# The second feed-forward map of two layers: a plain product by 32 contraction tiles against seven half-block products with operand sums on VectorE

## The chip, the cores and the metric

The program runs on one core of one Trainium2 chip. The metric is device microseconds of one execution, as a median over executions; lower is better. One profiled execution gives the trace. Engines are named as in the profile: PE is TensorE, PEld its weight loads, DVE is VectorE, ACT is ScalarE, POOL is GpSimd, SP is SyncE, whose queue issues nearly all DMAs.

## The reference, cut to what matters

The model is one attention block followed by two layers (a state-space mixer and an attention mixer), each with the feed-forward map below, on 1024 positions of width 1024, in fp32. Only the product with `w2` is computed in another way by the change.

```python
D_FF = 4 * D_MODEL                      # 4096, D_MODEL is 1024
def sq_relu_mlp(h, w1, w2):
    return jnp.square(jax.nn.relu(h @ w1)) @ w2
...
for layer in range(DEPTH_2):            # 2
    ...
    h = layer_norm(DN_ALPHA * h + mix, ln_mix_g[layer], ln_mix_b[layer])
    h = layer_norm(DN_ALPHA * h + sq_relu_mlp(h, w_ff1[layer], w_ff2[layer]), ln_ffn_g[layer], ln_ffn_b[layer])
```

## The kernel before

All fp32 products are made of three matmuls: each operand is split into a high part (ACT copies it to fp32r, line 157) and a low part (source minus high part, line 159, on POOL unless the call names DVE), and high x high, high x low and low x high are summed in PSUM. On-chip data lives in 46 pages (48 late in the program) of 128 x 1024 fp32, handed out from a queue: the page that was freed first is taken first, and whoever writes it waits until its last reader is done.

**First map (`ff1`, `ff1_unit`).** It already works by half-blocks: 16 units, each of two 128-row hidden tiles by 1024 positions, each of seven products of 12 matmuls (`product`, line 1276). A unit evicts its sums into two pages h0 and h1 (lines 1325 to 1363), squares them (line 1309) and stores the two tiles in DRAM (`self.dh`, lines 1357 and 1365). The four operand sums of a unit's weights are made on DVE (lines 1292 to 1295).

**Second map (`ff`).** The 32 hidden tiles are contracted in blocks of two (the last block of layer 1 has four). For a block the SP queue loads the hidden tiles and the rows of `w_ff2` (`wload`, line 165), ACT and POOL split them. For each of eight position tiles t, 12 matmuls of 128 x 512 (line 172) fill a PSUM pair of banks, and DVE adds it into a page z[t] (line 1425). In the last block the layer norm follows tile by tile (`ln`, with POOL's help). In layer 0 the last block is interleaved with transposes of finished tiles (`to_T`) and the first products of the attention mixer (`mla_front`); `mla_tables` computes rotary tables on DVE, ACT and POOL beside block 12. In layer 1 `last_rows` ends the program.

Order of the work: each engine runs its own instructions strictly in one order. The order is fixed when the program is built, by a scheduler that works from the order of the code, priorities and its own estimates. The SP queue is one of these ordered lists: a DMA whose source is not ready holds back every DMA behind it.

Of the kernel before, what the change touches and what calls it, by code (L numbers as in the profile page):

```python
# [59 lines left out]
class Kern:  # L60

    FB = [0, 4, 6, 0, 4, 6, 0, 0]
    FLAG = 5
# [1325 lines left out]

    def ff(self, X, units, layer, last):  # L1390
# [5 lines left out]
        z = []  # L1396
        f0 = 0
        for b, n in enumerate(sizes):
            end = b == len(sizes) - 1
            hid = [self.wload(self.dh[f0 + f]) for f in range(n)]  # L1400
            ws = [self.wload(i["w_ff2"][layer, f0 + f]) for f in range(n)]
            if b == len(sizes) - self.TB and not last:
                self.mla_tables()
            if end:
                gb = self.ln_rows(2 + layer)
                if not last:
                    self.psum(big=self.FB, tr=[2], kv=[4, 5], kq=[6, 7])
                    front, ahead = self.mla_front(), deque()
                    next(front)
            for t in range(8):  # L1410
                sl = slice(t * 128, (t + 1) * 128)
                if b == 0:
                    z.append(self.pg())
                    nc.sync.dma_start(z[t].t, self.dzr[t])
                ps = self.big()
                if last and end and t == 7:
                    self.last_rows(z[t].t, ps, hid, ws, sl, gb)
                    break
                for f in range(n):
                    (h, l), w = hid[f], ws[f]  # L1420
                    for a, c in ((h, 0), (h, 1), (l, 0)):
                        for hf in range(2):
                            cs = slice(hf * 512, (hf + 1) * 512)
                            self.mm(ps[:, cs], a[:, sl], w[c][:, cs], f == 0 and a is h and c == 0, f == n - 1 and a is l)
# [1 line left out]
                if end:
                    self.ln(z[t].t, gb, nc.gpsimd if t in ((5, 6) if last else (0, 1, 2, 3, 4, 5, 6)) else None)
                    if last:
                        nc.sync.dma_start(self.out.rearrange("(k t) d -> k t d", t=8)[:, t, :], z[t].t)
                    else:  # L1430
                        self.dump("h2", [(np.s_[t::8, :], z[t].t)])
                        nc.sync.dma_start(self.dres[:, t, :], z[t].t)
                        hT = [self.pg((128, 8, 128), F32R) for _ in range(2)]
                        self.to_T(z[t].t, *([p.t] for p in hT))
                        self.fr(z[t])
                        ahead.append((t, hT))
                        if len(ahead) > self.FLAG:
                            front.send(ahead.popleft())
            self.fr(*(p for w in hid + ws for p in w.pg))
            f0 += n  # L1440
# [1 line left out]
        if last:
            return
        for a in ahead:
            front.send(a)
        return front.send(None)

    def last_rows(self, z, ps, hid, ws, sl, gb):
# [3 lines left out]
        st, mv = self.sm(12, "st"), self.sm(2, "mv")  # L1452
        n = len(hid)
        for hf in range(2):
            cs = slice(hf * 512, (hf + 1) * 512)
            for f in range(n):
                (h, l), w = hid[f], ws[f]
                for a, c in ((h, 0), (h, 1), (l, 0)):
                    self.mm(ps[:, cs], a[:, sl], w[c][:, cs], f == 0 and a is h and c == 0, f == n - 1 and a is l)
            V.scalar_tensor_tensor(z[:, cs], ps[:, cs], IALPHA, z[:, cs], MUL, ADD)  # L1460
            V.bn_stats(st[:, hf * 6:hf * 6 + 6], z[:, cs])
# [373 lines left out]
```

## Time and profile before

| | |
|---|---|
| median of 3 runs | 3126.07 us (3124.21 to 3129.84) |
| the profiled execution's own time | 3125.07 us |
| its span in the trace | 3123.3 us |
| PE busy | 3002.7 us, 96% of the span |
| DVE, ACT, POOL busy | 54%, 35%, 44% of the span |
| mean granted TensorE clock | 0.983 of full |

Busy shares are over the whole program. What a stage costs is read from the engine whose wait ends last there. Times in the trace count from the start of the span.

### The profile page before, as it was taken

Reading aid. Unit: us, or ns where it says so; the run is one execution under the profiler, and the core shown is the slowest. Engines: PE = TensorE matmul, PEld = TensorE weight load, DVE = VectorE, ACT = ScalarE, POOL = GpSimd, SP = SyncE. Lnnn points to the kernel's source line nnn. Section 1 sums busy time; section 2 is a strip of 40 time slices with the busy share of each in tenths; the row PEclk is TensorE's granted clock in tenths of the full one; section 3 lists DMA queues with packets and bytes.
Section 4 is the critical chain, followed back from the end, with each engine's and each line's share of the span. In section 5 each row is a group of like instructions: output and inputs, shape, how many; then the busy total and the mean of one; then the engine's idle time right before and its main releaser. Section 6 shows DMA issues by size and latency. Waiting matters only on the chain.

```text
span 3123.3 us, 38309 instructions
## 1 busy us (share of the span) xinstructions
PE 3002.7 (96%) x14764; PEld 2471.2 (79%) x14764; DVE 1688.7 (54%) x2506; ACT 1106.9 (35%) x1723; POOL 1388.0 (44%) x831
## 2 busy tenths in 40 slices
PE   7999889999998899999999999999999899999998
PEld 6777667777777788878888888888998788888887
DVE  7555547755289401764444464756554854444446
ACT  4332247765233311332232211336662432232210
POOL 5454637644522233334456443513353354464442
PEclk9999999999999999999999999999999999999999
DMA  4353463476644112223353222110123233262211
GB/s 165 131 176 111 129 200 96 124 221 205 203 136 141 41 61 108 101 101 109 114 223 118 111 97 73 70 46 33 45 94 123 104 116 111 109 251 92 108 68 74
DMA packets 166168, 369.96 MB, mean 118 GB/s; under 512 B 21697, under 2 KB 71105, under 8 KB 165985
## 3 DMA queue, kind: packets, MB, share of 16 engines
q1 hardware_dynamic: 165840, 367.38, 34.8%
q8 instruction: 116, 1.90, 0.3%
q14 instruction: 68, 0.55, 0.1%
q10 hardware_dynamic: 144, 0.13, 0.0%
HBM read 252.90 MB, written 106.17 MB: 115 GB/s over the span
## 4 chain that ended last, share of the span: by engine, by line
PE 77%; DVE 11%; DMA 4%; issue 2%; POOL 2%; ACT 2%; SPq 0%; DVEq 0%; POOLq 0%; ACTq 0%
PE ps L172 56%; PE ps L1276 18%; DMA dr<-p 2%; POOL p L159 1%; PE ps L1648 1%; DMA p<-dr 1%; DVE p L1032 1%; DMA p<-in_w_ff 1%; DVE p L159 1%; DVE p L1045 1%; PE ps L668 1%; DVE p L498 1%; POOL rsd L180 1%; PE ps L521 1%; ACT p L500 1%
## 5 line engine op out<-in xcount | busy, mean ns | idle before, releaser
L172 PE MATMUL ps<-p,p 128*128 128x512 f32 (+6 forms) x10520 | 2238.1, 373 | 64.4 <-POOL p L159 12.1
L172 PEld LDWEIGHTS ps<-p,p 128*128 128x128 f32 (+2 forms) x10520 | 1790.5, 186 | 440.2 <-issue 50.1
L159 POOL TENSOR_TENSOR p<-p,p 128x1024 fp32r<-128x1024 f32 (+2 forms) x400 | 917.8, 2314 | 997.7 <-ACT p L157 687.9
L157 ACT ACTIVATE p<-p 128x1024 fp32r<-128x1024 f32 (+2 forms) x462 | 423.8, 939 | 935.8 <-DMA p<-in_w_ff 442.9
L1276 PE MATMUL ps<-p,p 128*128 128x512 f32 x2688 | 624.9, 393 | 17.6 <-ACT p L157 12.6
L1276 PEld LDWEIGHTS ps<-p,p 128*128 128x128 f32 x2688 | 506.4, 189 | 133.4 <-ACT p L157 14.1
L1425 DVE SCALAR_TENSOR_TENSOR p<-ps,p 128x1024 f32<-128x1024 f32 x247 | 301.3, 1223 | 335.1 <-PE ps L172 335.1
L180 POOL TENSOR_TENSOR rsd<-rst,nhalf 128x1 f32<-128x1 f32 (+1 forms) x64 | 102.9, 1610 | 219.7 <-DVE rst L178 219.6
L498 DVE CUSTOM_DVE_ANT_0 p<-ps,bw 128x1024 f32<-128x1024 f32 x64 | 77.4, 1220 | 30.6 <-PE ps L172 21.9
L1309 DVE SCALAR_TENSOR_TENSOR p<-p 128x512 f32<-128x512 f32 x96 | 90.3, 940 | 2.4
L1124 DVE SCALAR_TENSOR_TENSOR p<-p,ps 128x1024 f32<-128x1024 f32 x8 | 9.8, 1222 | 143.5 <-ACT p L1123 143.5
L500 ACT ACTIVATE p<-p,m 128x1024 f32<-128x1024 f32 x64 | 73.4, 1148 | 30.6 <-DVE m L498 19.4
L1642 POOL TENSOR_SCALAR p<-p,rz 128x256 f32<-128x256 f32 (+6 forms) x64 | 48.7, 762 | 66.3 <-DVE rz L1641 61.2
L513 POOL TENSOR_TENSOR p<-p,p 128x1024 f32<-128x1024 f32 x32 | 76.8, 2405 | 2.0
L512 POOL TENSOR_SCALAR p<-p,c 128x1024 f32<-128x1024 f32 x32 | 37.0, 1157 | 84.8 <-DMA dr<-p 43.5
L1363 DVE TENSOR_TENSOR p<-p,ps 128x512 f32<-128x512 f32 x32 | 22.0, 688 | 88.7 <-PE ps L1276 88.5
L1329 DVE TENSOR_TENSOR p<-p,ps 128x512 f32<-128x512 f32 x32 | 21.9, 685 | 87.2 <-PE ps L1276 87.2
L665 POOL TENSOR_SCALAR p<-p,rz 128x384 f32<-128x384 f32 x64 | 38.2, 602 | 68.9 <-DVE rz L664 55.1
L1652 DVE TENSOR_TENSOR p<-ps,p 128x512 fp32r<-128x512 f32 (+3 forms) x96 | 50.9, 553 | 32.2 <-ACT p L1651 31.3
L1637 POOL CAST p<-zeros 128x128 fp32r<-128x128 f32 x64 | 18.2, 295 | 105.1 <-PE ps L172 71.0
L1177 ACT ACTIVATE p<-ps 128x512 f32<-128x512 f32 x32 | 17.5, 594 | 130.1 <-PE ps L1176 130.0
L159 DVE TENSOR_TENSOR p<-ps,p 128x1024 fp32r<-128x1024 f32 (+1 forms) x42 | 42.3, 1017 | 38.6 <-ACT p L157 35.7
(252 smaller groups left out, 2396.5 us busy)
## 6 DMA issues: line engine op xcount, KB each, us to landing
p<-dr SPq DMA_DIRECT2D x174, 512.0 KB
dr<-p SPq DMA_DIRECT2D x158, 512.0 KB
p<-in_w_ff SPq DMA_DIRECT2D x136, 512.0 KB
bw<-in_rpbw SPq DMA_DIRECT2D x16, 768.0 KB
dr<-p SPq DMA_DIRECT2D x80, 128.0 KB
p<-p SPq DMA_DIRECT2D x64, 128.0 KB
p<-dr SPq DMA_DIRECT2D x32, 256.0 KB
p<-in_w_glu SPq DMA_DIRECT2D x16, 512.0 KB
```

Source lines behind the costliest of these rows:

```text
L157: nc.scalar.activation(hi, src, AF.Copy, scale=scale)
L159: (eng or nc.gpsimd).tensor_tensor(lo, src, hi.bitcast(F32), SUB)
L172: self.nc.tensor.matmul(out, l, r, start=start, stop=stop)
L180: nc.gpsimd.tensor_tensor(dst, t, self.nhalf[:, :n], ALU.pow)
L498: V.tensor_tensor_reduce(out=s.t, in0=ps, in1=bw[:, 896 - 128 * t:1920 - 128 * t], scale=-1.0, scalar=3e38, op0=ADD, op1=ALU.min, accum_ou ...
L500: A.activation(s.t, s.t, AF.Exp, bias=m[:, c:c + 1], scale=-1.0, accum_out=z[:, c:c + 1])
L513: G.tensor_tensor(p[0].t, p[0].t, p[1].t, ADD)
L1276: self.nc.tensor.matmul(ps, w[a][:, kt, :], x[b][kt // 2].t[:, kt % 2, :], start=start and kt == 0 and (a, b) == (0, 0), stop=kt == 3 and ...
L1309: V.scalar_tensor_tensor(h, h, 0.0, h, ALU.max, MUL)
L1425: V.scalar_tensor_tensor(z[t].t, ps, IALPHA, z[t].t, MUL, ADD)
L1642: G.tensor_scalar(s.t[:, :n], s.t[:, :n], rz, 1.0, MUL, MUL)
L1652: V.tensor_tensor(atl[kq][:, :nb, qi * 128:(qi + 1) * 128], tv, oh.bitcast(F32), SUB)
```

## The change

The second map of each layer is done by seven products of half-blocks instead of eight. Hidden tiles, positions and output columns are each cut in two: the 32 hidden tiles into even and odd, the positions into the first and second 512, the 1024 output columns into halves. With A the hidden activations (blocks by position half and tile parity) and B the rows of `w_ff2`, the sums of blocks of A are made once, in `ff1_unit` (four added DVE instructions of 128 x 512, lines 1368 to 1371 of the new file), and seven blocks instead of four are stored in DRAM (`self.da`). `ff2_ops` makes an operand of a step: it loads the pages, makes the sums of B on DVE, and splits all of them with ACT and DVE (no longer POOL). The steps are 4 sweeps k over 8 pairs of tiles j; k = 0, 1, 2 do two products each (banks P and R, 48 matmuls a step), k = 3 one (24 matmuls). A product's sums stay in four PSUM banks over a whole sweep, and are added into the z pages only at its end; the P banks are carried on from sweep to sweep. Steps are prepared two ahead in the order of the code (`AHEAD`). A sum of B needed in two sweeps goes through DRAM (`dv`, `dt4`). The layer norms of the first four position tiles stand inside sweep 3, without POOL; those of the last four follow the last sweep.

```diff
-    FB = [0, 4, 6, 0, 4, 6, 0, 0]
-    FLAG = 5
-    TB = 4
+    AHEAD = 2
@@ ff1_unit
-        nc.sync.dma_start(self.dh[2 * i + 1], h1.t)
-        self.fr(h1)
+        for p, c in ((1, lo), (2, hi)):
+            nc.sync.dma_start(self.da[p, i], h1.t[:, c])
...
-        nc.sync.dma_start(self.dh[2 * i], h0.t)
-        self.fr(h0)
+        s, t = self.pg(), self.pg()
+        V.tensor_tensor(s.t[:, lo], h0.t[:, hi], h1.t[:, hi], ADD)
+        V.tensor_tensor(s.t[:, hi], s.t[:, lo], h0.t[:, lo], SUB)
+        V.tensor_tensor(h0.t[:, hi], h0.t[:, lo], h0.t[:, hi], SUB)
+        V.tensor_tensor(t.t[:, lo], h1.t[:, lo], s.t[:, hi], SUB)
+        for p, a in ((0, h0.t[:, lo]), (5, h0.t[:, hi]), (3, s.t[:, lo]), (4, s.t[:, hi]), (6, t.t[:, lo])):
+            nc.sync.dma_start(self.da[p, i], a)
+        self.fr(h0, h1, s, t)
@@ new: ff2_ops
+        def sp(p):
+            h = [self.pg((128, 2, 512), F32R) for _ in range(2)]
+            self.split(p.t, h[0].t, h[1].t, eng=V)
+            return h
+        if k == 0:
+            p, q, b11, b21 = a(0), a(1), b(0, 0), b(1, 0)
+            ops = [(sp(p), sp(b11)), (sp(q), sp(b21))]
+            V.tensor_tensor(b21.t, b21.t, b11.t, SUB)
+            nc.sync.dma_start(self.dv[j], b21.t)
+        elif k == 1:
+            b11, b12, q, b22, p = b(0, 0), b(0, 1), a(3), b(1, 1), a(4)
+            V.tensor_tensor(b12.t, b12.t, b11.t, SUB)
+            V.tensor_tensor(b22.t, b22.t, b12.t, SUB)
+            ops = [(sp(p), sp(b22)), (sp(q), sp(b12))]
+        elif k == 2:
+            b12, b22, p, q = b(0, 1), b(1, 1), a(5), a(6)
+            v = self.pg((128, 2, 512))
+            nc.sync.dma_start(v.t, self.dv[j])
...
+            V.tensor_tensor(b12.t, b22.t, b12.t, SUB)
+            ops = [(sp(p), sp(b12)), (sp(q), sp(b22))]
+            V.tensor_tensor(v.t, v.t, b12.t, SUB)
+            nc.sync.dma_start(self.dt4[j], v.t)
+        else:
+            p, v = a(2), self.pg((128, 2, 512))
+            nc.sync.dma_start(v.t, self.dt4[j])
...
+            ops = [(sp(p), sp(v))]
@@ ff
-        self.psum(big=[0, 2, 4, 6])
-        sizes = [2] * 14 + [4] if last else [2] * 16
...
-                V.scalar_tensor_tensor(z[t].t, ps, IALPHA, z[t].t, MUL, ADD)
...
+            for kt in range(2):
+                for x, y in ((0, 0), (0, 1), (1, 0)):
+                    nc.tensor.matmul(ps[c][t], a[x].t[:, kt, t * 128:(t + 1) * 128], b[y].t[:, kt, :],
...
+            for t in range(4):
+                zs = z[4 * r + t].t[:, h * 512:(h + 1) * 512]
+                V.scalar_tensor_tensor(zs, ps[c][t], IALPHA, zs, MUL, ADD)
...
+        for k in range(3):
+            for j in range(8):
+                ops = ahead.popleft()
+                fetch()
+                if k == 1 and j == 0 and not last:
+                    self.mla_tables()
+                for c, op in enumerate(ops):
+                    for t in range(4):
+                        mms(c, op, t, j == 0 and (k == 0 or k == 1 and c == 1), j == 7)
+                    self.fr(*op[0], *op[1])
```

The orders below show three places. Up to the first units of layer 0's first map no engine's order differs. In the changed file line numbers differ: 157 is the split's low part (159 before), 170 the matmul of `mm`, 1276 the first map's products as before, 1310 the square, 1330, 1351, 1357 and 1364 the first map's evictions (1329, 1350, 1356, 1363 before), 1293 to 1296 the sums of weights, 1368 to 1371 the four new sums, 1408, 1436 and 1444 the loads of `ff2_ops`, 1426, 1430, 1431, 1438, 1440 its sums, 1427 and 1441 its stores, 1471 the second map's matmuls, 1479 its evictions.

First place: DVE in the middle of the first map of layer 0. Before, from the last eviction of one unit (L1363) to that of the next:

```order
L1363 TENSOR_TENSOR p_1038_10111<-p_1038_10111,ps 128x512
L1309 SCALAR_TENSOR_TENSOR p_1038_10111<-p_1038_10111 128x512
L1292 TENSOR_TENSOR p_1058_10342<-p_1056_10340 128x512
L1294 TENSOR_TENSOR p_1057_10341<-p_1052_10263,p_1056_10340 128x512
L1293 TENSOR_TENSOR p_1057_10341<-p_1058_10342,p_1052_10263 128x512
L1295 TENSOR_TENSOR p_1058_10342<-p_1052_10263,p_1057_10341 128x512
L1350 TENSOR_TENSOR p_1055_10297<-p_1055_10297,ps 128x512
L1309 SCALAR_TENSOR_TENSOR p_1055_10297<-p_1055_10297 128x512
L1329 TENSOR_TENSOR p_1064_10359<-p_1064_10359,ps 128x512
L1356 TENSOR_TENSOR p_1055_10297<-p_1055_10297,ps 128x512
```

The same in the change:

```order
L1364 TENSOR_TENSOR p_1048_10167<-p_1048_10167,ps 128x512
L1310 SCALAR_TENSOR_TENSOR p_1048_10167<-p_1048_10167 128x512
L1368 TENSOR_TENSOR p_1067_10363<-p_1048_10167,p_1054_10239 128x512
L1369 TENSOR_TENSOR p_1067_10363<-p_1067_10363,p_1048_10167 128x512
L1370 TENSOR_TENSOR p_1048_10167<-p_1048_10167 128x512
L1371 TENSOR_TENSOR p_1068_10364<-p_1054_10239,p_1067_10363 128x512
L1351 TENSOR_TENSOR p_1069_10374<-p_1069_10374,ps 128x512
L1310 SCALAR_TENSOR_TENSOR p_1069_10374<-p_1069_10374 128x512
L1295 TENSOR_TENSOR p_1086_10554<-p_1079_10465,p_1085_10553 128x512
L1293 TENSOR_TENSOR p_1087_10555<-p_1085_10553 128x512
L1357 TENSOR_TENSOR p_1069_10374<-p_1069_10374,ps 128x512
L1330 TENSOR_TENSOR p_1078_10437<-p_1078_10437,ps 128x512
```

The four new sums take the place right behind the unit's last eviction; the weight sums move behind the next eviction, and belong to a later unit than before.

Second place: DVE at the border of the first and second map of layer 0. Before:

```order
L1363 TENSOR_TENSOR p_1155_11227<-p_1155_11227,ps 128x512
L1309 SCALAR_TENSOR_TENSOR p_1155_11227<-p_1155_11227 128x512
L1425 SCALAR_TENSOR_TENSOR p_1169_11365<-ps,p_1169_11365 128x1024
L1425 SCALAR_TENSOR_TENSOR p_1170_11380<-ps,p_1170_11380 128x1024
L1425 SCALAR_TENSOR_TENSOR p_1171_11395<-ps,p_1171_11395 128x1024
```

In the change, from the fourth instruction behind the first map's last eviction (ahead of these stand that eviction, L1364, one split, L157, and one square, L1310):

```order
L157 TENSOR_TENSOR p_1230_11596<-p_1225_11587,p_1229_11595 128x1024
L1426 TENSOR_TENSOR p_1204_11533<-p_1204_11533,p_1203_11531 128x1024
L1368 TENSOR_TENSOR p_1187_11506<-p_1183_11382,p_1186_11448 128x512
L157 TENSOR_TENSOR p_1236_11608<-p_1228_11593,p_1235_11607 128x1024
L1369 TENSOR_TENSOR p_1187_11506<-p_1187_11506,p_1183_11382 128x512
L1370 TENSOR_TENSOR p_1183_11382<-p_1183_11382 128x512
L157 TENSOR_TENSOR p_1234_11604<-p_1226_11589,p_1233_11603 128x1024
L157 TENSOR_TENSOR p_1218_11562<-p_1213_11553,p_1217_11561 128x1024
L1371 TENSOR_TENSOR p_1188_11507<-p_1186_11448,p_1187_11506 128x512
L1426 TENSOR_TENSOR p_1228_11593<-p_1228_11593,p_1227_11591 128x1024
L157 TENSOR_TENSOR p_1232_11600<-p_1227_11591,p_1231_11599 128x1024
L157 TENSOR_TENSOR p_1222_11570<-p_1214_11555,p_1221_11569 128x1024
```

Pages 1201 to 1204 are raw pages of step j = 0, 1213 to 1216 of j = 1, 1225 to 1228 of j = 2; the last row makes the low part that step j = 1 needs, and DVE comes to it behind the four sums of the last unit and splits of step j = 2.

Third place: the SP queue in the middle of the second map of layer 0. Before, loads alone:

```order
L165 DMA p_1258_12271<-in_w_ff 128x1024
L165 DMA p_1261_12381<-dr_8628 128x1024
L165 DMA p_1264_12387<-dr_8628 128x1024
L165 DMA p_1291_12649<-in_w_ff 128x1024
L165 DMA p_1270_12399<-in_w_ff 128x1024
```

In the change, in sweep k = 2 (dr_11525 is `dv`, dr_11526 `dt4`, dr_8628 `da`):

```order
L1441 DMA dr_11526<-p_1432_12850 128x1024
L1408 DMA p_1443_12923<-dr_8628 128x2x512
L1408 DMA p_1444_12925<-dr_8628 128x2x512
L1436 DMA p_1445_12927<-dr_11525 128x1024
L1408 DMA p_1455_12998<-in_w_ff 128x2x512
L1408 DMA p_1467_13073<-in_w_ff 128x2x512
L1441 DMA dr_11526<-p_1445_12927 128x1024
L1408 DMA p_1456_13000<-dr_8628 128x2x512
```

Five loads now stand between two stores, each store waits for a DVE sum of a page that the third of these loads brings, and the loads of the next step stand behind it.

## Rows read from the trace of the kernel before

**Rows 1.** The page: span, busy time by engine, granted clock in 40 slices, chain.

```profile
span 3123.3 us, 38309 instructions
PE 3002.7 (96%) x14764; PEld 2471.2 (79%) x14764; DVE 1688.7 (54%) x2506; ACT 1106.9 (35%) x1723; POOL 1388.0 (44%) x831
PEclk9999999999999999999999999999999999999999
PE 77%; DVE 11%; DMA 4%; issue 2%; POOL 2%; ACT 2%; SPq 0%; DVEq 0%; POOLq 0%; ACTq 0%
```

**Rows 2.** Windows: first map, second map, layer 0's end; then layer 1's maps.

```profile
core 0: us, PE busy (x) PEld busy (x) DVE busy (x) ACT busy (x) POOL busy (x), PEclk, DMA share, GB/s
1360.00:1600.00 240.00, 240.00 (x1055) 197.68 (x1054) 111.63 (x139) 73.70 (x101) 115.36 (x50) 1.00 0.32 114
1640.00:1840.00 200.00, 200.00 (x878) 164.43 (x877) 91.64 (x76) 44.60 (x42) 107.56 (x46) 1.00 0.32 115
1966.00:2055.00 89.00, 85.05 (x519) 81.22 (x518) 54.19 (x118) 34.17 (x64) 43.16 (x35) 1.00 0.18 67
2500.00:2740.00 240.00, 239.90 (x1050) 196.78 (x1049) 113.53 (x139) 73.32 (x102) 114.73 (x51) 1.00 0.32 113
2775.00:3060.00 285.00, 285.00 (x1256) 235.31 (x1255) 130.16 (x107) 55.02 (x52) 135.40 (x57) 1.00 0.27 99
```

**Rows 3.** Waits of PE, second map of layer 0, then behind it.

```profile
PE ps L172 <- DVE p L1425: 1.2, 1, 1.2
...
PE ps L172 <- DVE p L1425: 1.7, 1, 1.7
PE ps L1164 <- DVE rst L178: 1.6, 1, 1.6
PE ps L1164 <- DVE mv L1144: 0.7, 1, 0.7
```

**Rows 4.** Timeline of PE where layer 1's second map starts, and DVE at its end.

```profile
2757.60 4.24 PE L172 MATMUL ps<-p,p 128*128 128x512 f32 x18
2761.68 5.61 PE L1276 MATMUL ps<-p,p 128*128 128x512 f32 x24
...
3113.26 0.69 DVE L1460 SCALAR_TENSOR_TENSOR p<-ps,p 128x512 f32<-128x512 f32 x1
```

**Rows 5.** Groups by form, 1400 to 1600 us (first map): busy us, mean ns, idle before.

```profile
L1276 PE MATMUL ps<-p,p 128*128 128x512 f32 x880 | 200.7, 390 | 0.0
L159 POOL TENSOR_TENSOR p<-p,p 128x1024 fp32r<-128x1024 f32 x31 | 78.2, 2550 | 21.3 <-ACT p L157 21.3
L1293 DVE TENSOR_TENSOR p<-p,p 128x512 f32<-128x512 f32 x10 | 17.8, 1781 | 0.0
L1294 DVE TENSOR_TENSOR p<-p,p 128x512 f32<-128x512 f32 x10 | 6.8, 685 | 0.0
```

**Rows 6.** Timeline of DVE, one unit of the first map.

```profile
1502.59 0.69 DVE L1363 TENSOR_TENSOR p<-p,ps 128x512 f32<-128x512 f32 x1 [3.48 <-PE ps L1276]
1503.31 0.69 DVE L1309 SCALAR_TENSOR_TENSOR p<-p 128x512 f32<-128x512 f32 x1
...
1510.10 0.69 DVE L1350 TENSOR_TENSOR p<-p,ps 128x512 f32<-128x512 f32 x1 [1.88 <-ACT p L1346]
1510.82 0.86 DVE L1309 SCALAR_TENSOR_TENSOR p<-p 128x512 f32<-128x512 f32 x1
1516.34 0.69 DVE L1329 TENSOR_TENSOR p<-p,ps 128x512 f32<-128x512 f32 x1 [4.65 <-PE ps L1276]
```

**Rows 7.** Timeline of DVE, page-wide two-operand work with POOL idle.

```profile
1332.07 1.21 DVE L1243 TENSOR_TENSOR p<-p,p 128x1024 f32<-128x1024 f32 x1
1334.41 1.21 DVE L159 TENSOR_TENSOR p<-p,p 128x1024 fp32r<-128x1024 f32 x1
```

**Rows 8.** Groups by form, 1640 to 1960 us (second map, layer 0).

```profile
L1425 DVE SCALAR_TENSOR_TENSOR p<-ps,p 128x1024 f32<-128x1024 f32 x119 | 145.0, 1224 | 163.2 <-PE ps L172 163.2
L159 POOL TENSOR_TENSOR p<-p,p 128x1024 fp32r<-128x1024 f32 x58 | 138.4, 2411 | 146.8 <-PE ps L172 81.6 <-ACT p L157 64.7
L157 ACT ACTIVATE p<-p 128x1024 fp32r<-128x1024 f32 x52 | 55.2, 1062 | 204.4 <-DMA p<-in_w_ff 132.6 <-DMA p<-dr 40.9 <-PE ps L172 26.4
```

**Rows 9.** DMA: the crowded border (window row), a store of 2 KB rows in 40 slices of 222.8 to 227 us, a lone load in the chain.

```profile
1612.00:1640.00 28.00, 27.91 (x121) 21.95 (x119) 9.86 (x11) 12.14 (x14) 16.17 (x7) 1.00 1.01 392
...
GB/s 0 0 0 0 0 0 0 0 0 332 390 351 371 449 390 332 390 410 410 351 390 332 98 0 0 0 0 0 0 0 0 0 0 0 0 0 0 0 0 0
...
1307.97 4.19 DMA p<-in_w_ff
```

**Rows 10.** Groups by form, whole span: DVE sums beside busy POOL.

```profile
L1243 DVE TENSOR_TENSOR p<-p,p 128x1024 f32<-128x1024 f32 x16 | 25.7, 1627 | 0.0
```

**Rows 11.** Window in which `mla_tables` runs on DVE.

```profile
1847.00:1867.00 20.00, 18.40 (x21) 1.00 0.22 80
```

More of the change, by code (lines that the diff above doesn't have):

```diff
@@ L1393, in ff @@
         self.ff1(X, units, layer)
-        self.psum(big=[0, 2, 4, 6])
-        sizes = [2] * 14 + [4] if last else [2] * 16
[L1396 to L1424, printed above, removed]
-                V.scalar_tensor_tensor(z[t].t, ps, IALPHA, z[t].t, MUL, ADD)
[L1426 to L1440, printed above, removed]
@@ new lines, in ff, with fetch, mms @@
+        z = [self.pg() for _ in range(8)]
+        self.dv, self.dt4 = self.dr([8, 128, 2, 512]), self.dr([8, 128, 2, 512])
+        self.psum(**{f"{n}{t}": [4 * c + t] for c, n in enumerate("PR") for t in range(4)})
+        ps = [[self.bank(f"{n}{t}") for t in range(4)] for n in "PR"]
+        steps, ahead = [(k, j) for k in range(4) for j in range(8)], deque()
+        def fetch():
+            if steps:
+                ahead.append(self.ff2_ops(layer, *steps.pop(0)))
+        def mms(c, op, t, start, stop):
+            a, b = op
+            for kt in range(2):
+                for x, y in ((0, 0), (0, 1), (1, 0)):
+                    nc.tensor.matmul(ps[c][t], a[x].t[:, kt, t * 128:(t + 1) * 128], b[y].t[:, kt, :],
+                                     start=start and kt == 0 and (x, y) == (0, 0), stop=stop and kt == 1 and x == 1,
+                                     skip_group_check=True)
@@ new lines, in ff, with done, turn @@
+        gb = self.ln_rows(2 + layer)
+        self.psb["tr"] = cycle([4])
+        if not last:
+            front = self.mla_front()
+            next(front)
+        tail, queue = [], deque()
+        def done(t):
+            if last:
+                nc.sync.dma_start(self.out.rearrange("(k t) d -> k t d", t=8)[:, t, :], z[t].t)
+            else:
+                self.dump("h2", [(np.s_[t::8, :], z[t].t)])
+                nc.sync.dma_start(self.dres[:, t, :], z[t].t)
+        def turn(t):
+            hT = [self.pg((128, 8, 128), F32R) for _ in range(2)]
+            self.to_T(z[t].t, *([p.t] for p in hT))
+            self.fr(z[t])
+            queue.append((t, hT))
@@ new lines, in ff @@
+        for j in range(8):
+            (op,) = ahead.popleft()
+            fetch()
+            if last and j > 3:
+                tail.append(op)
+            else:
+                for t in range(4):
+                    mms(0, op, t, False, j == 7)
+                self.fr(*op[0], *op[1])
+            if j % 2 == 0:
+                self.ln(z[j // 2].t, gb)
+                done(j // 2)
+            elif not last:
+                turn(j // 2)
+        st = [self.sm(12, "sth") for _ in range(4)]
@@ new lines, in ff @@
+        for t in range(4):
+            V.bn_stats(st[t][:, 6:12], z[4 + t].t[:, 512:])
+        if last:
+            for t in range(4):
+                for n, op in enumerate(tail):
+                    mms(0, op, t, False, n == 3)
+                zs = z[4 + t].t[:, :512]
+                V.scalar_tensor_tensor(zs, ps[0][t], IALPHA, zs, MUL, ADD)
+                if t < 3:
+                    self.ln(z[4 + t].t, gb, st=st[t])
+                    done(4 + t)
+            self.last_rows(z[7].t, st[3], gb)
+            return
@@ L1441, in ff, with last_rows @@
+        add(0, 1, 0)
+        self.psum(tr=[4, 2], kv=[6, 0], kq=[7, 1])
+        for t in range(4, 8):
+            self.ln(z[t].t, gb, st=st[t - 4])
+            done(t)
+            front.send(queue.popleft())
+            if t > 4:
+                turn(t - 1)
+        turn(7)
+        for a in queue:
+            front.send(a)
         self.fr(*gb)
[L1442 to L1445, printed above, removed]
         return front.send(None)
-    def last_rows(self, z, ps, hid, ws, sl, gb):
+    def last_rows(self, z, st, gb):
@@ L1450, in last_rows @@
         nc = self.nc
         V = nc.vector
[L1452 to L1461, printed above, removed]
+        mv = self.sm(2, "mv")
@@ L1462, in last_rows @@
+        V.bn_stats(st[:, 0:6], z[:, :512])
         V.bn_aggr(mv, st.rearrange("p (n s) -> p n s", s=6))
```

34 lines of the change are left out of this document (30 added, 4 removed).

## Prediction

> **What bounds the kernel now.** I read the page first: PE is busy for 96% of the span at a granted clock of 9 tenths or more in every slice, and 77% of the chain that ended last is PE [rows 1]. The windows say the same of the stages in question: PE is busy for 240 of 240 us in the middle of the first map, 200 of 200 in the second map of layer 0 and 285 of 285 in that of layer 1, all at the full granted clock (2.4 GHz) [rows 2]. The waits of PE in layer 0's second map come to a single one of 1.2 us [rows 3]. So in both second maps time is the number of matmuls times the pitch at which PE takes them, and everything else hides, as long as it keeps up.
>
> The pitch comes from layer 1, where nothing else is mixed in. Its second map starts at 2757.60, 24 matmuls of the first map (5.61 us) lie inside it, and the program's last eviction, DVE's half-page one at 3113.26, starts as the last matmul ends [rows 4]. 3113.26 - 2757.60 - 5.61 = 350.0 us for 32 tiles x 8 positions x 6 = 1536 matmuls: 0.228 us each. The duration of one in the groups (390 ns) is no pitch, since matmuls overlap. The first map, whose matmuls are already of the new form (six or more half-block matmuls in a row into one bank, a new weight load for each), shows 200.7 us for 880, again 0.228 [rows 5]. I take 0.228 for the new matmuls too.
>
> **What is removed on PE.** Seven half-block products of 8 pairs x 4 tiles x 6 = 192 matmuls are 1344 in place of 1536. 192 fewer at 0.228 us is 43.8 us a layer, **-87.6 us** for both. A step of two products is then 48 x 0.228 = 10.9 us, a step of sweep 3 is 5.5 us.
>
> **What the others must do in a step.** DVE first. It loses 128 page evictions a layer at 1.22 us [rows 8], 157 us, and does 28 half-page evictions instead (0.69 us for such an instruction [rows 6], 19 us). It gains all splits and sums. A page-wide two-operand instruction takes 1.21 us when POOL is idle [rows 7], and a mean of 1.63 where POOL works beside it [rows 10]. The splits leave POOL, where they cost 2.41 us each [rows 8], and POOL has almost nothing left in this stage, so I take 1.21. Sweep 0 needs four splits and a sum a step, 6.1 us; sweeps 1 and 2 four splits and two sums, 7.3 us; sweep 3 two splits, 2.4 us. All below PE's 10.9 and 5.5, and at 1.63 still (8.2, 9.8, 3.3). ACT makes as many high parts: 4 x 1.06 = 4.2 us a step [rows 8]. The heaviest sweep is k = 1 of layer 0, beside which the rotary tables run: 58 us of steps, at most 18.4 us for the tables [rows 11], 5.5 us of evictions: 82 of 87.5 us. It fits with little to spare.
>
> The row on contention first: in one stretch the same kind of half-page sum takes 1.78 us when it falls on POOL's splits and 0.69 when not [rows 5]. The Trainium skill, GPSIMD Engine Reference, section Specifications, says that GpSimd's SBUF interfaces are shared with VectorE and that DVE instructions with two SBUF inputs contend. By this rule, with which the trace agrees, the second map's sums run at the lone price and the first map's four new ones at up to the stretched one.
>
> DMA. A page of 512 KB moves in 1.34 us at the 392 GB/s of the crowded border [rows 9]. The new pages have rows of 2 KB instead of 4; a store of such rows ran at 330 to 450 GB/s in its 13 full slices [rows 9], some 1.4 us a page, so I take no extra cost for short rows. Sweeps 0 and 1 move five pages a step (6.7 to 7 us), sweep 2 six (8 to 8.4 us), of 10.9. The SP queue in sweep 2 is tighter than its bytes: from one store to the next stand the store itself, two loads, the load of `dv`, the sum that needs it. Four transfers of 1.34 us, the fixed part of a lone load (4.19 less 1.34 [rows 9]), a sum and up to two splits ahead of it: 5.4 + 2.9 + 3.6 = 11.9 us, a microsecond more than a step. Over eight steps that is 8 us, and the work enters the sweep two to three steps (22 to 33 us) ahead, since the pages of a step are free once PE is through with the step four before it (8 of 48 hold z, a step holds 8 and up to 5 raw). I take 0 and keep 8 a layer.
>
> **Bank edges.** At the end of a sweep DVE empties eight banks, 5.5 us. PE needs the P banks again behind the 24 matmuls of R (5.5 us), and P's four evictions take 2.8. So they hide; splits that stand between them can cost something. I take 0.5 us for each of six edges, +3 us (bounds 0 and 3 each).
>
> **First map.** Each unit gets four half-page sums, 2.8 us at 0.69, 7.1 at 1.78. DVE is busy for 111.6 of 240 us there [rows 2], 8.9 of a unit's 19.1. In the unit shown, the last eviction and its square end at 1504.0 and the next eviction is due at 1510.1 [rows 6]; between them stood the weight sums, which the new order moves behind that eviction, at 1511.7, where DVE was idle until 1516.3. The four sums end at 1506.8, or 1511.1 if stretched. Nobody on PE waits for them: their readers come a sweep later. Seven stores of 256 KB replace two of 512 KB, 1.8 MB in 19 us. Cost 0; without that cover, 2.8 us a unit, 88 us in all.
>
> **The border of the maps.** Before, PE lost almost nothing. Now the DVE order has 15 instructions from the last first-map eviction to the low part that step 1 needs: five half-page ones at 0.69 (the eviction and four sums), a square, seven splits and two sums at 1.21: 3.5 + 0.7 + 10.9 = 15.1 us. PE meanwhile has step 0 and twelve matmuls of step 1, 58 to 60 x 0.228 = 13.2 to 13.7 us. It waits 1.4 to 1.9 us. Loads may add: some 20 pages (z, three steps) are 27 us of DMA within a stretch that begins some 20 us ahead of the border. I take 3 us a layer, **+6 us**, bounds 0 and 10 each.
>
> **Ends.** In layer 0 PE waited 4.0 us for DVE's layer norms behind the map and 1.2 inside [rows 3]. Now four tiles are normalised inside sweep 3 and give PE four tiles of mixer products (some 8 us each) while DVE does the other four. I take **-3 us** (0 to -5.2). In layer 1 the last tile's eviction, statistics and output follow the last matmul as before: 0. Sweep 3 there has 14 us of splits, 5.5 of evictions and some 20 of layer norms in 44: it holds.
>
> **Sum**, against the profiled execution's own 3125.1 us: -87.6 + 6 - 3 + 3 = -81.6, so 3043.5. The median of the runs is 1 us above that execution; I predict **3044 us**.
>
> **Rivals.**
> 1. *The SP queue paces sweep 2* (or loads late at the borders pace sweep 0). For: stores wait on DVE with the next loads behind them; 11.9 against 10.9. Against: the lead, and DMA's mean share of 0.32 so far [rows 2]. If a load takes 1 us longer and the lead is gone, 13 us a step: 2.1 x 16 = 33 us, 3077.
> 2. *DVE becomes the bound.* For: it is the engine with all new work, in one fixed order, where one late page holds all. Against: 7.3 of 10.9. At 1.63 only sweep 1 of layer 0 fails: 78 + 18 + 6 = 102 us against 87.5: 3059.
> 3. *The first map pays, and the kernel is slower.* If the four sums delay the evictions so that PE waits for all of them in each of 32 units, 32 x 2.8 = 88 us: 3132. It decides from 2.6 us a unit on. For: POOL works there, and DVE's order is fixed. Against: the idle time around 1508 and 1512 to 1516.
> 4. *The change saves nothing on PE*: a pitch of 0.260 for the new form would eat all. The first map's 0.228 speaks against it.
>
> **How the numbers follow.** Forecast 0.68 (3032 to 3056), rival 1 0.13, rival 2 0.08, rival 3 0.05 with milder forms of it 0.04 (up to 3120), rival 4 0.02. The lower end is everything hidden, 3125.1 - 87.6 - 5.2 = 3032; the upper takes in rivals 1 and 2 and half-way forms of 3: 3031 to 3085. A difference of 0.2% (6 us) is about what a measurement of this kernel can tell. Faster 0.93, same 0.02, slower 0.05.
>
> **What would show it.** Right: 1344 matmuls of line 1471 a layer at 0.228 us and no wait of PE inside sweeps; at the borders one wait of some 2 us for a split on DVE; first-map units still 19.1 us apart. Wrong: waits of PE for splits in sweep 2 with SP waiting for the sum of line 1440 (rival 1); DVE busy all through sweep 1 of layer 0 (rival 2); PE below 240 of 240 in the first map (rival 3); a longer pitch (rival 4).

## The result and the profile after

The changed kernel takes 3057.63 us (median of 4 runs, 3052.07 to 3059.8), the kernel before 3125.76: a ratio of 0.9777 (0.976 to 0.9794). It is faster by 68 us; 3044 was forecast, in 3031 to 3085. The profiled execution took 3052.07 us; its page, span and engines (answers to [rows 1]):

```profile
span 3050.3 us, 38397 instructions
PE 2917.8 (96%) x14380; PEld 2403.1 (79%) x14380; DVE 1879.5 (62%) x2754; ACT 1188.6 (39%) x1810; POOL 1053.8 (35%) x694
```

384 matmuls are gone, DVE has more work and POOL less, as planned. Where the time went is read by stretches. The view of one line gives its matmuls with their first and last start; here the first and the second map of each layer in the changed kernel:

```profile
L1276 PE MATMUL ps<-p,p x1344: 387/389/796, 1304.0 to 1639.9; 128*128 128x512 f32 x192
L1471 PE MATMUL ps<-p,p x1344: 387/389/504, 1636.9 to 1948.8; 128*128 128x512 f32 x192
...
L1276 PE MATMUL ps<-p,p x1344: 387/389/796, 2401.8 to 2733.6; 128*128 128x512 f32 x192
L1471 PE MATMUL ps<-p,p x1344: 387/389/504, 2730.6 to 3041.5; 128*128 128x512 f32 x192
```

A first map is counted from its first to its last start plus one pitch, less 0.228 us for each matmul of the second map inside it: 1639.9 + 0.2 - 1304.0 - 2 x 0.228 = 335.7.

| stretch, us | before | changed | difference | forecast |
|---|---|---|---|---|
| up to the first map of layer 0 | 1305.6 | 1304.0 | -1.6 | 0 |
| first map, layer 0 | 322.8 | 335.7 | +12.9 | 0 |
| second map of layer 0, mixer, up to the first map of layer 1 | 811.3 | 762.1 | -49.2 | -42.3 |
| first map, layer 1 | 323.3 | 331.6 | +8.3 | 0 |
| second map, layer 1 | 350.0 | 308.4 | -41.6 | -39.3 |
| behind the last matmul | 10.3 | 8.6 | -1.7 | 0 |

The forecast puts 43.8 us a layer of saved matmuls, 3 of border and 1.5 of bank edges into the second maps. The first row is the noise of an execution: no instruction there differs, and over the profiled executions below the first map starts between 1301 and 1313 us. So the lengths of maps are compared below, beside medians; the kernel before, run again beside each group of experiments, had medians of 3125.4 to 3129.9 us.

The second maps came out as forecast or better. The first maps, which were to cost nothing, took 21.2 us more than before. The windows of layer 0's first map (changed kernel; answers to the first row of [rows 2]) show PE short of full, and DVE at 156.6 us in place of 111.6:

```profile
1360.00:1600.00 240.00, 234.75 (x1013) 191.08 (x1012) 156.59 (x185) 70.70 (x99) 111.43 (x50) 0.99 0.44 150
```

The chain of waits from 1370 to 1402 us ends in a wait of PE of 2.75 us (start, duration, what):

```profile
1385.44 0.32 SPq L1373
...
1385.81 0.02 SPq L1313
...
1385.86 4.58 DMA p<-in_w_ff
...
1390.53 0.69 DVE p L1294
1391.22 0.60 DVE p L1295
1391.82 2.80 DVE p L1296
1394.62 0.61 DVE p L1364
...
1395.26 2.20 DVE p L1310
...
1397.48 0.70 DVE p L1368
...
1398.20 1.94 DMA dr<-p
1400.13 0.63 ACT p L155
1400.76 0.50 ACT p L1347
...
1401.30 0.79 PE ps L1276
```

Read downwards: the SP queue is through with the stores of a unit's sums (L1373) at 1385.8, and only then issues the load of the next weight tile (L1313). DVE waits for that load, makes the weight sums, and behind them, in its fixed order, the eviction, the square and the first of the four new sums. The store of that page must land (1.94 us) before ACT may write a split into a page that becomes free with it; behind that split stands ACT's eviction L1347, for which PE waits. One of these weight sums took 2.80 us and the square 2.20, where the kernel before has 0.69 for such an instruction that does not fall on POOL's splits [rows 5, rows 6], so DVE's own time is in this wait too. Two links of this loop the change makes longer: loads stand behind stores that wait for the sums (a link of order), and splits get pages that the sums and their stores hold (a link of pages). Which counts, or whether DVE's time alone does, is what most experiments ask.

The loss is not spread evenly over the units. Layer 0's map is 8.0 us behind the kernel before by its 467th matmul (of 1344), layer 1's 7.2 us by its 387th; from there 504 and 752 matmuls, some six and nine units, run without a wait of PE:

```profile
1434.57 114.65 PE L1276 MATMUL ps<-p,p 128*128 128x512 f32 x504 [0.26 <-ACT p L1341]
...
2513.22 170.85 PE L1276 MATMUL ps<-p,p 128*128 128x512 f32 x752 [0.35 <-ACT p L1341]
```

What else is lost comes at the end of the maps, most of it in the last unit, at the border.

### The profile page after: what moved, and what is told of

Same layout as the page of the kernel before. It is cut to its first block, busy times and chain, and to the rows that moved or that the text cites. A ratio compares the mean times of both kernels' runs of the same rounds, so it can differ in the third digit from the quotient of the medians.

```text
span 3050.3 us, 38397 instructions
## 1 busy us (share of the span) xinstructions
PE 2917.8 (96%) x14380; PEld 2403.1 (79%) x14380; DVE 1879.5 (62%) x2754; ACT 1188.6 (39%) x1810; POOL 1053.8 (35%) x694
## 4 chain that ended last, share of the span: by engine, by line
PE 55%; DVE 10%; DMA 5%; issue 3%; POOL 2%; ACT 1%; SPq 0%; DVEq 0%; POOLq 0%; ACTq 0%
PE ps L170 23%; PE ps L1471 19%; PE ps L1276 10%; DMA p<-in_w_ff 3%; POOL p L157 1%; DMA p<-dr 1%; PE ps L1753 1%; DVE p L1030 1%; DVE p L157 1%; DVE p L1310 1%; DVE p L1043 1%; ACT p L155 1%; DMA dr<-p 1%; DVE p L1154 0%; DVE p L1036 0%
## 5 line engine op out<-in xcount | busy, mean ns | idle before, releaser
L170 PE MATMUL ps<-p,p 128*128 128x512 f32 (+6 forms) x7448 | 1532.1, 365 | 62.9 <-POOL p L157 11.7
L170 PEld LDWEIGHTS ps<-p,p 128*128 128x128 f32 (+2 forms) x7448 | 1214.5, 185 | 311.4 <-issue 50.3
L157 POOL TENSOR_TENSOR p<-p,p 128x1024 fp32r<-128x1024 f32 (+2 forms) x272 | 604.5, 2235 | 946.5 <-ACT p L155 861.2
L155 ACT ACTIVATE p<-p 128x1024 fp32r<-128x1024 f32 (+2 forms) x558 | 520.9, 959 | 959.0 <-DMA p<-in_w_ff 160.3
L1276 PE MATMUL ps<-p,p 128*128 128x512 f32 x2688 | 631.8, 396 | 31.8 <-ACT p L155 12.4
L1276 PEld LDWEIGHTS ps<-p,p 128*128 128x128 f32 x2688 | 509.2, 191 | 151.8 <-ACT p L155 14.7
L1471 PE MATMUL ps<-p,p 128*128 128x512 f32 x2688 | 613.0, 390 | 3.4 <-DVE p L1479 1.6
L1471 PEld LDWEIGHTS ps<-p,p 128*128 128x128 f32 x2688 | 503.6, 188 | 110.6 <-issue 2.4
L157 DVE TENSOR_TENSOR p<-p,p 128x1024 fp32r<-128x1024 f32 (+1 forms) x286 | 315.4, 1129 | 109.7 <-ACT p L155 108.6
L1310 DVE SCALAR_TENSOR_TENSOR p<-p 128x512 f32<-128x512 f32 x96 | 116.6, 1214 | 2.2
L496 DVE CUSTOM_DVE_ANT_0 p<-ps,bw 128x1024 f32<-128x1024 f32 x64 | 77.3, 1219 | 30.7 <-PE ps L170 21.2
L1295 DVE TENSOR_TENSOR p<-p,p 128x512 f32<-128x512 f32 x32 | 34.8, 1088 | 75.0 <-DMA p<-in_w_ff 75.0
L157 DVE TENSOR_TENSOR p<-ps,p 128x1024 fp32r<-128x1024 f32 (+1 forms) x42 | 42.0, 1015 | 39.9 <-ACT p L155 37.2
```

Source lines behind the costliest of these rows:

```text
L155: nc.scalar.activation(hi, src, AF.Copy, scale=scale)
L157: (eng or nc.gpsimd).tensor_tensor(lo, src, hi.bitcast(F32), SUB)
L170: self.nc.tensor.matmul(out, l, r, start=start, stop=stop)
L496: V.tensor_tensor_reduce(out=s.t, in0=ps, in1=bw[:, 896 - 128 * t:1920 - 128 * t], scale=-1.0, scalar=3e38, op0=ADD, op1=ALU.min, accum_ou ...
L1276: self.nc.tensor.matmul(ps, w[a][:, kt, :], x[b][kt // 2].t[:, kt % 2, :], start=start and kt == 0 and (a, b) == (0, 0), stop=kt == 3 and ...
L1310: V.scalar_tensor_tensor(h, h, 0.0, h, ALU.max, MUL)
```

## The experiments

Lengths are us. The last three columns are of the profiled execution: first maps of the layers, second map of layer 1.

| kernel | median | ratio to before (95%) | first map 0 | first map 1 | second map 1 |
|---|---|---|---|---|---|
| changed kernel | 3057.6 | 0.9777 (0.976 to 0.9794) | 335.7 | 331.6 | 308.4 |
| e1, sums in place | 3066.4 | 0.9812 (0.9794 to 0.983) | 339.6 | 345.0 | 304.7 |
| e2, no sums, no s and t | 3026.5 | 0.9672 (0.9653 to 0.9691) | 321.4 | 319.9 | 309.1 |
| e3, no sums, idle pages | 3073.4 | 0.9824 (0.9808 to 0.984) | 342.1 | 348.2 | 308.3 |
| e4, splits on POOL | 3124.1 | 0.9983 (0.9966 to 1.0) | 335.5 | 329.0 | 336.8 |
| f1, in place and ring | 3046.0 | 0.9731 (0.9705 to 0.9757) | 334.4 | 329.1 | 304.7 |
| f2, f1 and four more sums | 3127.0 | 0.9998 (0.9982 to 1.0013) | 354.9 | 363.8 | 327.7 |
| f3, f1 and a page less | 3088.0 | 0.9871 (0.9845 to 0.9897) | 349.9 | 349.7 | 312.8 |
| g1, one step ahead | 3050.5 | 0.975 (0.9722 to 0.9779) | 335.2 | 329.7 | 306.0 |
| h1, f1 and earlier loads | 3026.3 | 0.9674 (0.966 to 0.9687) | 325.6 | 324.6 | 305.2 |
| h2, f1 with sums on POOL | 3155.5 | 1.0087 (1.0071 to 1.0103) | 375.3 | 373.3 | 320.6 |
| p1, earlier loads alone | 3039.5 | 0.9718 (0.9701 to 0.9735) | 328.8 | 325.5 | 305.9 |
| p2, h1, ring of six, one ahead | 3048.6 | 0.9745 (0.9722 to 0.9768) | 328.4 | 329.1 | 309.4 |

**e1: sums over h0 and h1.**

```diff
-        s, t = self.pg(), self.pg()
-        V.tensor_tensor(s.t[:, lo], h0.t[:, hi], h1.t[:, hi], ADD)
+        V.tensor_tensor(h1.t[:, hi], h0.t[:, hi], h1.t[:, hi], ADD)
...
-        self.fr(h0, h1, s, t)
+        self.fr(h0, h1)
```

> The four sums of the first map are written over h0 and h1 instead of into two new pages s and t, and the two halves that are overwritten are stored earlier; the same four DVE instructions and the same seven stores stay. In the changed kernel the two first maps take 20.8 us more than before (335.7 and 331.5 us against 322.9 and 323.4). Page theory (two more pages in a unit let the page of the previous unit's h1 come to the next unit's w4 split on ACT, which must wait for the last sum; ACT's evictions stand behind it): the pages freed earlier come to that split, the loss falls to 0 to 6 us, time 3037 to 3044. DVE theory (the sums' own time delays the evictions): the same loss, 3052 to 3060. Store theory (seven stores instead of two hold up the weight loads): the same, 3052 to 3060.

Slower than the changed kernel by 9 us, against all three theories. Its chain shows a loop that closes on itself every 19.7 us, where PE needs 19.1:

```profile
1443.82 0.70 DVE p L1371
1444.54 2.01 DMA dr<-p
1446.57 0.03 SPq L1313
...
1446.63 3.47 DMA p<-in_w_ff
...
1463.52 0.70 DVE p L1371
1464.24 2.01 DMA dr<-p
1466.27 0.03 SPq L1313
```

Fewer pages are no help by themselves: pages are handed out in turn, and now the weight load itself gets a page that waits for the last store. The page theory in its first form (too many pages in a unit) is wrong; it matters who gets which page.

**e2: no sums, and no s and t.** **e3: no sums, but s and t taken and given back unused.**

```diff
-        V.tensor_tensor(s.t[:, lo], h0.t[:, hi], h1.t[:, hi], ADD)
...
+        for p, a in ((0, h0.t[:, lo]), (5, h0.t[:, hi]), (3, h1.t[:, hi]), (4, h0.t[:, hi]), (6, h1.t[:, lo])):
```

> Leaves out the four sums of the first map and the pages s and t; the same seven stores are made, from h0 and h1 as they are, so what the second map multiplies is not the right operands, with the same instructions otherwise. Page theory: first maps back at 323 us each, 3037 us, equal to the in-place kernel. DVE theory: 3037 too, but 10 us or more below the in-place kernel. Store theory: the loss of 20.8 us stays, 3052 to 3060.

> The kernel without the four sums, but with the two pages s and t taken from the queue and given back at the same places, unused. Page theory: without any sum, the w4 split again gets the previous unit's h1 page and now waits for the stores out of it; some 10 to 20 us of the loss come back, 3047 to 3060. DVE theory: no sums, no loss, equal to the kernel without sums (within 3 us). Store theory: as the kernel without sums, both slow.

Without the sums and their two pages the first maps cost nothing, with all seven stores made: bytes and number of stores are not it. The pages are handed out as in e1, so the sums make the difference between e2 and e1 (18 and 25 us; two stores also stand elsewhere). But e3 has no sums either and loses 21 and 28 us against e2, by pages alone, 10.4 and 11.5 of it at the border of the maps: from 1380 to 1620 us ACT's splits waited there 13 times, 50 us in all, for stores to land (second row). With s and t in place the sums were thus not taken out by themselves without another loss.

```profile
ACT p L155 <- DVE p L1294: 110.7, 12, 10.5
ACT p L155 <- DMA dr<-p: 50.1, 13, 4.7
```

**f1: e1 with the pages of h0 and h1 in a ring of their own.** **f2: four more DVE sums a unit on top of f1, into a page nobody reads.**

```diff
+    def hp(self):
+        i = (self.hfree or self.free).popleft()
...
-        h0 = self.pg()
+        h0 = self.hp()
```

> The in-place kernel with the pages of h0 and h1 in a ring of their own (four pages), so that no page of a weight waits for a unit's sums or for the stores out of it; the same DVE sums and the same seven stores on the SP queue. In the in-place kernel a unit took 19.7 to 19.9 us in a closed chain: sums, store landed (2.0 us), the page free, load of the next weights (3.5 us), weight sums, splits, evictions, squares, sums. Page theory: without that link the unit is PE's 19.1 us again, first maps 320 to 324 us each, time 3026 to 3036. Store-queue theory (the loads stand behind stores that wait for the sums, in SP's order): the chain is only 0.4 us shorter, the first maps stay at 335 to 345, 3052 to 3066. DVE theory (the sums' own time): 335 to 345 too.

> The kernel with the ring, with four more DVE sums of 128 x 512 in each unit of the first map, into one page of their own that nobody reads. Page theory: DVE has room for it (2.8 us at 0.69, at most 7 us stretched, of a unit's 19.1), first maps stay at 320 to 326 us, within 6 us of the kernel with the ring. DVE theory: each 2.8 us or more shows, 32 units, 3080 or more.

f1 is 20 us faster than e1, and its loss sits elsewhere: PE waits in the early units of layer 0, and no more inside the map from 1408 on. The SP queue in those units, then PE:

```profile
1360.11 4.57 SPq L1379 DMA_DIRECT2D dr<-p  x4
1365.74 0.33 SPq L1343 DMA_DIRECT2D p<-in_w_ff  x1
1366.44 0.33 SPq L1296 DMA_DIRECT2D p<-in_w_ff  x1
```

```profile
1372.36 33.01 PE L1280 MATMUL ps<-p,p 128*128 128x512 f32 x134 [5.30 <-ACT p L1354]
1407.31 222.63 PE L1280 MATMUL ps<-p,p 128*128 128x512 f32 x970 [1.94 <-DVE p L1358]
```

The loads are issued right behind four stores that waited for the sums. In f2 the added sums (four of 1.09 us on the mean, 4.4 us a unit) cost 20 and 35 us a map, 1.3 and 2.2 a unit, with DVE not full (199.6 of 240 us there). That fits sums on a loop with little slack, but f2 is not clean: its scratch page comes from the same rotation and moves who gets which page.

**h1: f1, with the loads of a unit's weights earlier in the code.** **p1: the same edit alone, on the changed kernel.**

```diff
+        else:
+            r1 = self.pg()
+            nc.sync.dma_start(r1.t, self.i["w_ff1"][layer, 2 * i + 1])
         yield
...
+        if early:
+            r0, r1 = self.pg(), self.pg()
+            nc.sync.dma_start(r0.t, self.i["w_ff1"][layer, 2 * i])
+            nc.sync.dma_start(r1.t, self.i["w_ff1"][layer, 2 * i + 1])
         yield
-        if early:
-            r0 = self.pg()
```

> The kernel with the ring, with the second weight tile of each unit of the first map loaded together with the first one, and both tiles of the early units loaded one step of the code earlier, so that on the SP queue fewer weight loads stand behind stores that wait for a unit's sums. In the kernel with the ring the first maps took 334.4 and 329.1 us; nearly all of the 17 us above before lie in the first units (PE waits of 5.3, 1.9, 2.3, 1.2 and 2.1 us, with the clock at half for some 4 to 7 us behind the longer ones), where the weight loads were issued at 1365.7, behind stores that waited until 1364.4 for DVE's sums. If SP's order is the link: these waits go, first maps 321 to 326 us each, time 3030 to 3038. If it is DVE's own time: first maps as before, 3043 to 3049.

> The changed kernel with the earlier weight loads alone: s and t as they were, no ring. If the order on the SP queue is by itself what the first map pays for: first maps at 324 to 327 us each, time 3038 to 3046. If the pages are needed too (w4's split still gets the page of the previous unit's h1, and one more page is taken early): no gain, first maps at 331 us or more, 3050 to 3065.

h1 is the fastest kernel, 31 us below the changed one and as fast as e2, which makes no sums at all. In p1, with the sums and s and t untouched, the earlier loads give 18 us in the median (10.4 between the two profiled executions) and 6.9 and 6.1 us of the first maps. DVE hardly waits for weights any more: from 1380 to 1620 us it waited for loads 12 times, 61.5 us in all, in the changed kernel, and once in p1 (second view); in the kernel before it was 8.0 us in 11 times.

```profile
DVE p L1295 <- DMA p<-in_w_ff: 37.2, 6, 6.6
DVE p L1293 <- DMA p<-in_w_ff: 21.0, 5, 5.0
DVE p L1294 <- DMA p<-in_w_ff: 3.3, 1, 3.3
```

```profile
DVE p L1292 <- DMA p<-in_w_ff: 4.7, 1, 4.7
```

ACT's wait for a page held by the last sum is still there, of p1 in the first row and of the changed kernel in the second (1380 to 1620 us: total, times, longest):

```profile
ACT p L155 <- DVE p L1375: 56.2, 12, 4.8
```

```profile
ACT p L155 <- DVE p L1371: 47.2, 11, 4.3
```

But not all of p1's gain undoes what the change cost. The first 134 matmuls of a map took 46.8 and 46.4 us before, 46.8 and 47.0 in the changed kernel and 42.5 in p1 (42.5 in h1 too): 8.8 us are won at the start of the maps, where the change had lost almost nothing. From there to the border the changed kernel lost 15.2 us and p1 7.4; at the border p1 lost 3.8 us more than the changed kernel. So the link of order carries about half of what was lost inside the maps. The earlier loads also take their pages earlier, so a part of this half can be due to pages; what the other half is (late pages, DVE's time) stays open.

The longest wait left in p1's first map of layer 0 that the kernel before did not have is at its end, the border:

```profile
1629.00 4.61 PE L1276 MATMUL ps<-p,p 128*128 128x512 f32 x12 [3.92 <-ACT p L1351]
```

**h2: the four sums on POOL.** (f1 with `nc.gpsimd` for `V` in the four sums.)

> The kernel with the ring, with the four sums of a unit on POOL instead of DVE (POOL's splits of 128 x 512 take 1.3 to 1.75 us, so some 6 us a unit, and POOL is busy for 9 of 19.1). If DVE's time is the link in the first units: first maps 321 to 326 us, 3030 to 3038. If what counts is when the sums are done (the stores wait for them, and the loads wait behind the stores): the sums end later, the loss grows by 10 us or more, 3055 or more; and POOL's work stretches DVE's squares further.

The slowest of all: PE loses 41 and 44 us a map against f1. SP's stores wait for POOL's sums, and the loads behind them; but POOL also makes the splits, and of the 43.2 us for which PE waited in layer 0's first map 22.2 ended with a split on POOL. DVE is relieved (121.6 of 240 us), and it does not help. So the run does not tell whether the late sums or the late splits cost more.

**f3: one page less in a unit** (weight sums over r0), **p2: ring of six pages and AHEAD = 1** on top of h1, **g1: AHEAD = 1** alone on the changed kernel.

```diff
-            V.tensor_tensor(sa.t[:, hi], r0.t[:, lo], r1.t[:, lo], SUB)
-            V.tensor_tensor(sb.t[:, hi], r0.t[:, hi], sa.t[:, lo], SUB)
+            V.tensor_tensor(r0.t[:, lo], r0.t[:, lo], r1.t[:, lo], SUB)
+            V.tensor_tensor(r0.t[:, hi], r0.t[:, hi], sb.t[:, hi], SUB)
```

> The kernel with the ring, and the sums of the first map's weights made over r0 as well, one page less in each unit (the products take the same operands, paired in other pages). If pages are still short behind the ring, the first maps gain up to 5 us each; if the ring already leaves PE as the only limit, within 3 us of the kernel with the ring.

> The kernel with the ring and the earlier loads, with a ring of six pages instead of four (in it ACT's first eviction of a unit still waited for a store to land, and PE 2.8 us for it), and with steps of the second map prepared one ahead (2.4 us shorter in layer 1's second map by itself). If both hold together: first maps 321 to 324 us, 3016 to 3024. If two pages less for the weights cost more than the ring gives: first maps 327 or more, 3028 or above.

> The changed kernel with steps of the second map prepared one ahead in the code instead of two. The prediction had sweep 2's SP queue at 11.9 us for a step of 10.9, hidden by a lead of two to three steps. If that loop is real and the lead hides it: PE waits in sweep 2, 8 to 33 us more in all, 3060 to 3090. If the queue keeps up by itself: within 6 us of the changed kernel except at the border, where one step less is ready (up to 5 us a layer).

f3 and p2 are misses: saving a page cost 42 us against f1, more pages for h0 and h1 with one step less of lead 22 us against h1. In f3 ACT's first eviction of a unit waited for stores to land (46.4 us in 6 times from 1380 to 1620 us), so another user of the rotation got a late page, as in e1; for p2 that is a guess. It was not tried which page it is, so their cause stays open. g1 shows the loop in sweep 2 to be no matter: with a step less of lead PE waits for nothing there, and the time is 7 us below the changed kernel's (the intervals overlap), not above it.

**e4: the second map's low parts on POOL again.**

```diff
-            self.split(p.t, h[0].t, h[1].t, eng=V)
+            self.split(p.t, h[0].t, h[1].t)
```

> The low parts of the second map's operands on POOL again (line 157 without eng=V), sums stay on DVE. POOL makes four low parts a step at 2.41 us = 9.6 of a step's 10.9 us, and two = 4.8 of 5.5 in sweep 3. If this part of the change does not matter: within 6 us of the changed kernel. If it does (a chain of ACT, POOL and the stretched sums on DVE, 1.63 us for each): POOL at 88% of a step loses some tens of us through waits at borders and beside the layer norms, 3070 to 3100.

All the gain is gone, more than either theory had. Groups of 1660 to 1900 us (sweeps 0 to 2 of layer 0), of e4 and then of the changed kernel (busy us, mean ns, idle before):

```profile
L157 POOL TENSOR_TENSOR p<-p,p 128x1024 fp32r<-128x1024 f32 x81 | 220.7, 2765 | 22.8 <-ACT p L155 22.8
L1471 PE MATMUL ps<-p,p 128*128 128x512 f32 x892 | 212.0, 400 | 28.3 <-DVE p L1479 20.3 <-POOL p L157 8.0
...
L1426 DVE TENSOR_TENSOR p<-p,p 128x1024 f32<-128x1024 f32 x7 | 23.6, 3391 | 32.8 <-POOL p L157 21.1 <-DMA p<-dr 11.7
```

```profile
L157 DVE TENSOR_TENSOR p<-p,p 128x1024 fp32r<-128x1024 f32 x86 | 103.1, 1218 | 55.1 <-ACT p L155 54.7
...
L1426 DVE TENSOR_TENSOR p<-p,p 128x1024 f32<-128x1024 f32 x5 | 6.1, 1221 | 0.1
```

A split on POOL takes 2.77 us beside DVE's sums, above the 2.41 of [rows 8], and the page-wide sums on DVE take 2.0 to 3.4 us instead of 1.22. Four such splits are 11.1 us, more than a step; POOL is the bound, and PE loses most at the ends of sweeps, where DVE evicts late. The rule of the Trainium skill, GPSIMD Engine Reference, section Specifications (DVE instructions with two SBUF inputs contend with GpSimd), holds here, on both engines.

## Why the prediction was right, and which step was not

The time lies in the stated range, just above the band of the forecast (3032 to 3056). What held is the main sum; what came beside it is a mild form of rival 3, to which the text gave 0.04 and for which the upper end of the range had room; the sign named for it came, PE at 234.75 of 240 us in the first map. The first maps' miss of 16.6 us is in part hidden in the total, since the ends, the edges and the tail came out better than forecast.

- **192 matmuls a layer at 0.228 us, -87.6.** Right. In layer 1, 720 in a row took 163.87 us, 0.2276 each; rival 4 did not occur.
- **DVE's price of 1.21 us a split with POOL idle.** Right: 1.218. DVE was busy for 165.5 us of the 240 from 1660 on, 7.5 a step of 10.9, and PE full; rival 2 did not occur, in sweep 1 of layer 0 either (66.6 of the 88 us from 1740 on).
- **SP queue in sweep 2, 0.** Right: the stores waited up to 7.6 us for the sums of line 1440, and PE for nothing; g1 needs no lead for it.
- **Border, +3 a layer.** The size was right (3.8 and 2.5 us), the place only in part. PE waited 0.95 us for DVE's split, as worked out (1.4 to 1.9), but 2.89 us before that, for ACT's eviction of the first map's last unit, which stood behind a split whose load came late. PE and ACT of the changed kernel:

```profile
1634.07 3.04 PE L1276 MATMUL ps<-p,p 128*128 128x512 f32 x12 [2.89 <-ACT p L1347]
...
1654.41 259.13 PE L1471 MATMUL ps<-p,p 128*128 128x512 f32 x1140 [0.95 <-DVE p L157]
```

```profile
1632.47 1.06 ACT L155 ACTIVATE p<-p 128x1024 fp32r<-128x1024 f32 x1 [3.22 <-DMA p<-dr]
1633.44 0.58 ACT L1347 ACTIVATE p<-ps 128x512 f32<-128x512 f32 x1
```

- **Layer 0's end, -3.** Mis-sized: some -6 to -7 (-49.2 + 43.7 for the matmuls, and the border's 0.95). All four waits of [rows 3], 5.2 us, are gone.
- **Bank edges, +3.** In size right: one wait of 1.65 us in layer 1, none above 0.2 in layer 0.
- **First map, 0. This step failed**, at "Nobody on PE waits for them: their readers come a sweep later." The sums' readers do come later, but their stores stand on the SP queue ahead of the next unit's weight loads, and their pages go to the next unit's splits. So the sums lie on a loop from one unit to the next. Of the 21.2 us, 4.6 are the border's waits above (2.89 and 1.75); the other 16.6 are 0.5 us a unit on the mean, not rival 3's 2.8 in each, and most of them (8.0 and 7.2) had fallen by the 467th and the 387th matmul of the maps, behind which units ran at PE's pace. The price of the sums was right: 0.69 us each from 1400 to 1600 us. The text weighed the stores by their bytes (1.8 MB in 19 us) and not by their place in the queue. Shown: with the sums and their two pages left out nothing is lost (e2), and the pages of e2 with the sums lose 38.5 us against the kernel before (e1). In the changed kernel itself the chain of its longest wait goes over both links, and earlier loads take back about half of what was lost inside the maps (p1). How much each link and DVE's time carry is open: h2 took the sums off DVE, but put them ahead of POOL's splits.
- **Behind the last matmul, 0.** -1.7: the last two instructions of line 1152 took 1.41 us, where before they took 3.38 beside POOL's page-wide work for the tile ahead.

Sum: -87.6, +6.3 border, about -6.5 end, +1.7 edge, +16.6 first maps, -1.7 tail, -1.6 noise ahead: -72.8, against -73.0 between the two spans.

## What to carry to other kernels

When work is added to an engine with idle time, follow what it delays besides its readers: its stores, the loads behind these in the same queue, and the pages that it holds. A loop from one tile to the next across load, sums, split and eviction shows in no busy share; the chain of waits shows it, and issuing the next tile's loads ahead of stores that wait for new work can give back time (3057.6 to 3039.5 us here, and to 3026.3 with a ring of pages for h0 and h1). Count where such a gain falls: here 8.8 us of it came at the start of the maps, where the kernel before took as long as the changed one. Pages handed out in turn couple unrelated work, so that one page less can make a kernel slower.
